# Two forgetting-attention heads by halves of their queries, with the first merged half's projection beside them

## The chip, the cores and the metric

One core of a Trainium2 chip runs the kernel. A time is the device time of one execution in microseconds. The engines are TensorE (PE, with its weight loads as PEld), VectorE (DVE), ScalarE (ACT), GpSimd (POOL) and SyncE (SP), which issues the DMA transfers. Each engine runs its own list of instructions in order and waits on semaphores for the others.

## The reference

A decoder block on 2048 tokens with 1024 channels in float32: a token mixer and a SwiGLU FFN. The change is in the token mixer, whose core is this:

```python
def token_mixer(h, w_in, b_forget, w_up_a, w_up_b, w_out):
    z = h @ w_in
    qa, ka, va, qb, kb, vb, fz, gza, gzb = jnp.split(z, SPLIT_POINTS, axis=-1)
    ya = dilated_mixture(qa, ka, va) @ w_up_a
    yb = forgetting_attention(qb, kb, vb, fz, b_forget) @ w_up_b
    merged = jax.nn.sigmoid(gza) * ya + jax.nn.sigmoid(gzb) * yb
    return merged @ w_out
```

Branch A (`dilated_mixture`) has 12 heads of 64 channels in three groups; each query sees a short band of keys, and the three groups are merged with weights made from their softmax denominators. Branch B (`forgetting_attention`) has 4 heads of 64 channels; each query sees all keys up to its own, with a bias that is a running sum of log forget gates. So of a head of branch B the second half of the queries needs all keys, the first half only the first half of them.

## The kernel before

float32 products are made of parts: a factor is split into a high and a low part (`split`, L106 on ACT for the high part, L107 on DVE for the low one), and `mm3` takes three products (L100, L101, L102). After the input projection the scheduler of the program gets five pieces of work in this order, as generators that yield after each step:

- `branch_a` (L711): 12 heads, each in four units of 512 queries: scores (L754, L758), eviction with bias and running maximum (L760), exponential (L768), transposes (L785), products with the values (L796), output rows `utok` (L808), stored to `u_scr`. With the last unit the softmax statistics of the group go out, and come back as `md`.
- `branch_b` (L912): heads 0 to 3, each whole (`head_f`, L820). A head loads queries `qs`, keys `kh` and `kl` (1 MB each) and values `vhl` (1 MB) through `head_tiles`, and has eight units of 256 queries (`cq`), of two blocks each. `scores(cq, b)` makes the products with the keys in segments of up to 512 (L850), the eviction with the bias `bi` (L852) and the exponential (L862). `sums(cq)` makes transposes (L886), splits them (`ph` by ACT, `pl` by DVE), and multiplies with the values (L894). Every second unit stores its 512 queries to `u_scr` and adds one to `f_done`.
- `merge_weights` (L946): the weights of branch A's three groups, on DVE and ACT, stored to `w_scr` (in the trace `wrow<-mw`, L970).
- `up(0)` and `up(1)` (L972): the projection of the first and the second half of the tokens. The first part builds the operand `y`: for each of four 128-row blocks it loads branch outputs (`uw<-u`, L981) and weights spread over partitions (`uw<-wrow` and `uw<-rc`, L987) into a `uw` tile, multiplies (L989), adds the groups (L991) and splits. The pool `bigx` holds three `uw` tiles, so the fourth load waits until the first tile has been used. The second part takes eight column blocks with 48 products each of 512 columns (L100 to L102, `psZ<-y,wu`), then multiplies with the gates (`gt`, L1014), adds and stores.

The multiplies and adds of the first part are put on engines by two tables, `UM` and `UA`: of 24, 14 run on POOL and 10 on DVE. `together` (L1018) interleaves generators by a virtual clock, one step of the one that is furthest behind, with a factor for each. First come branch A (`PACE[0]` = 0.6) and branch B; when A ends, `merge_weights`; then branch B alone until `f_done` is 14, which is when the first half of head 3's queries is done; then `up(0)` (`PACE[1]` = 0.6) beside what is left of head 3; then what is left of `up(0)`, and `up(1)`. This is the order in which work is given to the scheduler; it moves instructions on each engine by its own estimates, so that the order on an engine is to be read from the built program.

Of the kernel before, what the change touches and what calls it, by code (L numbers as in the profile page):

```python
# [11 lines left out]
F32R = mybir.dt.float32r  # L12
I32 = mybir.dt.int32
AF = mybir.ActivationFunctionType
ALU = mybir.AluOpType
# [3 lines left out]
P = 128  # L19
T = 2048  # L20
D = 1024
NT = T // P
# [27 lines left out]
UT = (("pc",), ("wh", "wl"))  # L50
UM = ("GVGG", "GVGV")
UA = ("GG", "VV")

PACE = (0.6, 0.6)

# [4 lines left out]
def trunk(ctx, tc, x, c, w_ada, b_ada, norm_mix, w_in, b_forget, w_up_a, w_up_b, w_out,  # L60
# [19 lines left out]
    def slot(tag, name, shape=None, dt=F32):  # L80
        kib, n = SLOTS[tag]
        return (sv if tag == "mid" else sb).tile(shape or [P, kib * 256], dt, tag=tag, name=name, bufs=n)
# [4 lines left out]
    def raw(t):  # L87
        return t.bitcast(F32)
# [580 lines left out]
    nev = [0]  # L669

    def head_tiles(qj, kj, half, vj, sl, d):

        r = []
        for n, j, part in (("qs", qj, 0), ("kh", kj, 0), ("kl", kj, 1)):
            r.append(slot("big", n, dt=F32R))
            to, src = raw(r[-1]), qk_scr[j][half, part:part + 2].rearrange("a p t -> (a p) t")
            if n == "qs" and d == 16:

                for c_ in range(NCH):
                    SP.dma_start(to.rearrange("p (r c n) -> p c r n", c=NCH, r=16)[:, c_],  # L680
                                 src[:, c_ * CH:(c_ + 1) * CH].rearrange("p (r n) -> p r n", r=16))
            else:
                SP.dma_start(to, src)
        full = vj < 3
        if full:
            vhl = slot("mid", "va", [P, NT, 65])
            G.memset(vhl[:, :, 64:65], 1.0)
        else:
            vhl = slot("big", "vhl", [P, NT, P], F32R)
        src = v_scr[vj][:, sl, :]  # L690
        dst = vhl[:, :, :64] if full else raw(vhl)
        if d == 1:
            SP.dma_start(dst, src.rearrange("(n i) e -> i n e", i=P))
        else:
            src = src.rearrange("(n i r) e -> n i r e", r=d, i=P)
            dst = dst.rearrange("p (r n) e -> n p r e", r=d)
            for n in range(NT // d):
                SP.dma_start(dst[n], src[n])
        return (*r, vhl)

# [118 lines left out]

    def head_f(h):  # L820
        qs, kh, kl, vhl = head_tiles(12 + h // 2, 14 + h // 2, h % 2, 3, h, 1)
        nf = [slot("mid", "nf") for _ in range(2)]
        for i in range(2):
            SP.dma_start(nf[i], brow(nf_scr[h, i * D:(i + 1) * D], D, P))
        uy, den, Ls = [None], {}, {}

        def scores(cq, b):
# [7 lines left out]
            for i, sg in enumerate(segs):  # L835
# [13 lines left out]
                for j, kk in enumerate((kh, kl)):  # L849
                    PE.matmul(s[:, :e - sg], qs[:, qb * P:(qb + 1) * P], kk[:, sg:e],  # L850
                              start=(j == 0), stop=(j == 1))
# [14 lines left out]
        def sums(cq):  # L866
# [9 lines left out]
            for kp in range(cq + 1):  # L876
# [14 lines left out]
                for i, kb in enumerate((2 * kp, 2 * kp + 1)):  # L891
                    q0 = P if last and i == 1 else 0
                    for j, p_ in enumerate(ops):
                        PE.matmul(uo[:, q0:256], vhl[:, kb, :], p_[:, 256 * i:256 * i + 256 - q0],  # L894
                                  start=(kp == 0 and i == 0 and j == 0),
                                  stop=(last and i == 1 and j == 1), skip_group_check=True)
            if cq % 2 == 0:
# [14 lines left out]
    def branch_b():  # L912

        behind = None
        for h in range(NHB):
            scores, sums = head_f(h)
            for cq in range(8):
                for b in range(2):
                    scores(cq, b)
                    yield (2 * cq + b + 1) / 4 * 0.7  # L920
                    if b == 0 and behind:
                        yield from behind()
                behind = lambda sums=sums, cq=cq: sums(cq)
            if h == NHB - 1:
                yield from behind()
    f_end, f_done = [None], [0]

# [44 lines left out]
    def up(cp):  # L972
# [3 lines left out]
        for p_ in range(4):  # L976
            acc = None
            for g in range(3 if p_ < 2 else 1):
# [7 lines left out]
                for i in range(2):  # L986
                    SP.dma_start(wb[64 * i:64 * i + 64, :],  # L987
                                 bass.AP(tensor=src.tensor, offset=src.offset + i * T, ap=[[0, 64], [1, D]]))
                (V if UM[cp][g + (p_ > 1) * 3] == 'V' else G).tensor_tensor(uu, uu, wb, op=ALU.mult)  # L989
                if acc is not None:  # L990
                    (V if UA[cp][g - 1] == 'V' else G).tensor_tensor(uu, uu, acc, op=ALU.add)  # L991
                acc = uu
            for c_ in range(2):
                split(y[c_][0][:, p_, :], y[c_][1][:, p_, :], acc[:, c_ * CH:(c_ + 1) * CH])
            yield 3.0
        for j in range(KT):
# [6 lines left out]
            for c_ in range(2):  # L1003
# [5 lines left out]
                for i, gt in enumerate(gts):  # L1009
                    o = ps("Z")  # L1010
                    for k in range(2 * i, 2 * i + 2):
                        mm3(o, w[:, 0, k, :], w[:, 1, k, :], yh[:, k, :], yl[:, k, :], k == 2 * i,
                            k == 2 * i + 1)
                    V.tensor_tensor(gt, o, gt, op=ALU.mult)  # L1014
# [16 lines left out]
    merge_weights()  # L1031
    together([(gb, 1.0)], lambda: f_done[0] >= 4 * (NHB - 1) + 2)
    tt_only[0] = "U"
# [181 lines left out]
```

## Time and profile before

| what | us |
|---|---|
| median of 3 runs | 2899.26 |
| lowest and highest run | 2895.91, 2902.61 |
| the profiled execution's own time | 2897.54 |
| its span, first to last instruction | 2895.8 |
| input projection, up to the first attention product | 0 to 880 |
| branches A and B beside each other | 880 to 1178.4 |
| branch B alone | 1178.4 to 1257.8 |
| `up(0)` beside the rest of head 3 | 1257.8 to 1342.7 |
| rest of `up(0)` and `up(1)` | 1342.7 to 1418.4 |
| output projection and FFN | 1418.4 to 2895.8 |

The bounds of the stages are the ends and starts of groups of PE's instructions: the last product of branch A (L796), the first of `up(0)` (L100), the last with branch B's values (L894) and the last of `up(1)` (L102). The table is read with the page's share of PE, which is busy for nearly the whole span, and with the busy time and granted clock by stage.

### The profile page before, as it was taken

The page shows a single profiled execution, that of the slowest core. Times are in us where ns is not written, and L with a number is a line of the kernel's source. Part 1 is how long each engine was busy: PE and PEld are TensorE (multiplying, and loading weights), DVE is VectorE, ACT ScalarE, POOL GpSimd, SP SyncE. Part 2 cuts the span into 40 slices and gives each one's busy share as a digit, 9 for nine tenths or more (in the row PEclk, how much of TensorE's full clock was granted, in tenths as well). Part 3 has the DMA queues.
Part 4 walks back from the last instruction along what each step waited for, and adds up shares of the span by engine and source line. Part 5 has one row for each costly group of instructions (what it writes and reads, how often), then busy time and mean ns, then how long its engine had stood idle before and what let it go on. Part 6 is the DMA issues. An engine that isn't in the chain of part 4 may idle for free.

```text
span 2895.8 us, 40840 instructions
## 1 busy us (share of the span) xinstructions
PE 2774.1 (96%) x13778; PEld 2309.5 (80%) x13778; DVE 2041.0 (70%) x4269; ACT 1376.4 (48%) x2726; POOL 213.9 (7%) x305
## 2 busy tenths in 40 slices
PE   7999999999999999888899999999999999989998
PEld 6789888978887878666677788888888888868876
DVE  5865578576646887687967766657755558795987
ACT  4654335344447777653356533335333335343543
POOL 0000000000002222563200000000000000000000
PEclk9999999999999999998999999999999999999999
DMA  7687466467757668569766554444522235785642
GB/s 242 166 226 220 131 207 204 148 168 212 235 176 261 239 176 259 144 176 310 265 211 207 189 178 138 135 146 137 164 86 79 83 109 179 217 264 168 219 155 99
DMA packets 520858, 530.52 MB, mean 183 GB/s; under 512 B 91556, under 2 KB 372540, under 8 KB 514236
## 3 DMA queue, kind: packets, MB, share of 16 engines
q1 hardware_dynamic: 520648, 527.91, 58.6%
q8 instruction: 108, 1.77, 0.3%
q14 instruction: 102, 0.84, 0.1%
HBM read 356.51 MB, written 171.29 MB: 182 GB/s over the span
## 4 chain that ended last, share of the span: by engine, by line
PE 47%; DVE 3%; ACT 1%; DMA 1%; issue 1%; DVEq 0%; ACTq 0%
PE psX L100 9%; PE psX L101 9%; PE psX L102 9%; PE psZ L100 4%; PE psZ L101 4%; PE psZ L102 4%; PE psY L101 2%; PE psY L102 2%; PE psY L100 2%; DVE wl L107 0%; DVE wt L217 0%; PE psT L1090 0%; ACT wh L106 0%; ACT u L244 0%; DMA wr<-act 0%
## 5 line engine op out<-in xcount | busy, mean ns | idle before, releaser
L106 ACT ACTIVATE wh<-wt 128x512 fp32r<-128x512 f32 (+1 forms) x464 | 288.5, 623 | 637.0 <-PE psX L101 344.6
L107 DVE TENSOR_TENSOR wl<-wt,wh 128x512 fp32r<-128x512 f32 (+1 forms) x464 | 314.6, 681 | 257.8 <-ACT wh L106 240.6
L106 ACT ACTIVATE wh<-wr 128x512 fp32r<-128x512 f32 (+1 forms) x324 | 201.5, 623 | 433.1 <-PE psX L101 239.1
L107 DVE TENSOR_TENSOR wl<-wr,wh 128x512 fp32r<-128x512 f32 (+1 forms) x324 | 220.0, 680 | 200.9 <-ACT wh L106 183.2
L217 DVE TENSOR_TENSOR wt<-wr 128x512 f32<-128x512 f32 (+1 forms) x216 | 146.5, 678 | 12.0 <-DMA wr<-in_w_in_dram 5.1
L217 DVE TENSOR_TENSOR wt<-wr,wt 128x512 f32<-128x512 f32 (+1 forms) x216 | 147.8, 684 | 3.8
L244 ACT ACTIVATE u<-psX 128x512 f32<-128x512 f32 x216 | 125.3, 580 | 8.1 <-PE psX L102 8.1
L838 POOL TENSOR_SCALAR bi<-nf,F_col 128x512 f32<-128x512 f32 (+3 forms) x160 | 104.9, 658 | 229.3 <-DVE mx L852 192.3
L862 ACT ACTIVATE L<-L,nmf 128x512 f32<-128x512 f32 (+3 forms) x160 | 103.1, 647 | 20.7 <-DVE nmf L858 20.5
L894 PE MATMUL psY<-ph,vhl 128*128 128x256 f32 (+1 forms) x288 | 82.4, 299 | 9.1 <-ACT ph L106 7.8
L1120 DVE TENSOR_TENSOR ac<-psZ,u 128x512 f32<-128x512 f32 x88 | 60.4, 687 | 42.2 <-PE psZ L102 41.2
L894 PE MATMUL psY<-pl,vhl 128*128 128x256 f32 (+1 forms) x288 | 81.8, 312 | 7.8 <-DVE pl L107 6.8
L106 ACT ACTIVATE ph<-psT 128x512 fp32r<-128x512 f32 (+1 forms) x101 | 56.2, 568 | 53.5 <-PE psT L886 53.3
L796 PE MATMUL psY<-pf,va 128*65 128x128 f32 (+1 forms) x408 | 77.7, 324 | 1.3 <-DVE pf L792 0.9
L760 DVE CUSTOM_DVE_ANT_0 L<-psX,bias 128x128 f32<-128x128 f32 (+1 forms) x192 | 64.6, 357 | 19.8 <-PE psX L758 14.1
L107 DVE TENSOR_TENSOR pl<-psT,ph 128x512 fp32r<-128x512 f32 (+1 forms) x101 | 64.5, 646 | 16.2 <-ACT ph L106 16.0
L768 ACT ACTIVATE L<-L,nm 128x128 f32<-128x128 f32 (+1 forms) x192 | 72.1, 450 | 5.5 <-DVE nm L763 4.5
L100 PE MATMUL psZ<-y,wu 128*128 128x512 f32 x128 | 55.7, 435 | 18.7 <-DVE gt L1014 11.5
L100 PE MATMUL psX<-f_A11h,wh 128*128 128x512 f32 x176 | 69.4, 394 | 0.0
L894 PEld LDWEIGHTS psY<-ph,vhl 128*128 128x128 f32 x288 | 56.7, 197 | 15.6 <-ACT ph L106 10.9
L102 PE MATMUL psX<-f_A11h,wl 128*128 128x512 f32 x176 | 69.1, 393 | 0.0
L101 PE MATMUL psX<-f_A11l,wh 128*128 128x512 f32 x176 | 69.1, 392 | 0.0
(536 smaller groups left out, 8732.6 us busy)
## 6 DMA issues: line engine op xcount, KB each, us to landing
x<-x SPq DMA_DIRECT2D x192, 256.0 KB
wr<-in_w_ffn_in_dram SPq DMA_DIRECT2D x88, 512.0 KB
wr<-in_w_in_dram SPq DMA_DIRECT2D x64, 512.0 KB
qk<-sh SPq DMA_DIRECT2D x192, 128.0 KB
act<-ac SPq DMA_DIRECT2D x88, 256.0 KB
pc<-wfg SPq DMA_DIRECT2D x77, 256.0 KB
qk<-st SPq DMA_DIRECT2D x128, 128.0 KB
wa<-in_w_ada_dram SPq DMA_DIRECT2D x64, 256.0 KB
```

The source lines that it names most:

```text
L100: PE.matmul(o, lh, rh, start=first, stop=False, skip_group_check=True)
L101: PE.matmul(o, lh, rl, start=False, stop=False, skip_group_check=True)
L102: PE.matmul(o, ll, rh, start=False, stop=last, skip_group_check=True)
L106: A.activation(hi, src, AF.Copy)
L107: V.tensor_tensor(lo, src, raw(hi), op=ALU.subtract)
L217: V.tensor_tensor(v[i], *made[i](g, v), op=ALU.subtract)
L244: A.activation(t, o, AF.Copy, scale=1.0 if scale is None else scale)
L768: A.activation(Lb(b, o0, 256), Lb(b, o0, 256), AF.Exp, bias=nm[:, bb:bb + 1])
L796: PE.matmul(uo[:65, qb_[0] * P:qb_[0] * P + w], va[:, 4 * u + kb_, :], pf[:, pos:pos + w], start=i_ == 0, stop=i_ == len(runs) - 1, skip_g ...
L838: G.tensor_scalar(bi[:, :e - sg], nf[sg // D][:, sg % D:sg % D + e - sg], 1.0, F_col[:, qb * NHB + h:qb * NHB + h + 1], op0=ALU.mult, op1= ...
L862: A.activation(Ls[cq, b, sg][:, :e - sg], Ls[cq, b, sg][:, :e - sg], AF.Exp, bias=nm, accum_out=dp[:, i:i + 1])
L894: PE.matmul(uo[:, q0:256], vhl[:, kb, :], p_[:, 256 * i:256 * i + 256 - q0], start=(kp == 0 and i == 0 and j == 0), stop=(last and i == 1 ...
```

## The change

Branch B is given in six pieces instead of four: heads 0 and 1 whole, then the first halves of the queries of heads 2 and 3, then their second halves. A first half loads 1024 queries and 1024 keys, two operands to a tile (`kk`, `qv`); a second half loads the other 1024 queries and all keys and values again. Heads 2 and 3 so load 5.5 MB each in place of 4 MB. `up(0)` may start when `f_done` is 12, with both first halves done, and runs beside both second halves; its factor `PACE[1]` is 1.25 in place of 0.6, and a step of its first part counts 4.0 in place of 3.0. The tables `UM` and `UA` go: all 24 multiplies and adds of the `uw` tiles run on DVE. The first products of `up(0)` (`cp + j + c_ + k == 0`) are held in the order behind the last product with branch B's values that has been given so far.

```diff
-PACE = (0.6, 0.6)
+PACE = (0.6, 1.25)
+
+FOX = ((None, 0), (None, 1), (0, 2), (0, 3), (1, 2), (1, 3))
...
+    def half_tiles(h, part):
+
+
+        qj, kj, half, n = 12 + h // 2, 14 + h // 2, h % 2, D if part == 0 else T
+        if part == 0:
+            t = [slot("big", "kk", dt=F32R), slot("big", "qv", dt=F32R)]
+            kh, kl = [t[0][:, i * D:(i + 1) * D] for i in range(2)]
+            qs, vhl = t[1][:, :D], t[1][:, D:].rearrange("p (n e) -> p n e", e=P)
+        else:
+            kh, kl, qs, vhl = [slot("big", nm, dt=F32R) for nm in ("kh", "kl", "qs", "vhl")]
+            qs, vhl = qs if part is None else qs[:, :D], vhl.rearrange("p (n e) -> p n e", e=P)
+        SP.dma_start(raw(qs), qk_rows(qj, half, 0)[:, D if part else 0:n])
+        for i, kk in enumerate((kh, kl)):
+            SP.dma_start(raw(kk), qk_rows(kj, half, i)[:, :n])
+        SP.dma_start(raw(vhl), v_scr[3][:n, h, :].rearrange("(n i) e -> i n e", i=P))
+        return qs, kh, kl, vhl
...
-                        PE.matmul(uo[:, q0:256], vhl[:, kb, :], p_[:, 256 * i:256 * i + 256 - q0],
-                                  start=(kp == 0 and i == 0 and j == 0),
-                                  stop=(last and i == 1 and j == 1), skip_group_check=True)
+                        f_pe[0] = PE.matmul(uo[:, q0:256], vhl[:, kb, :], p_[:, 256 * i:256 * i + 256 - q0],
+                                            start=(kp == 0 and i == 0 and j == 0),
+                                            stop=(last and i == 1 and j == 1), skip_group_check=True).ins
...
-        for h in range(NHB):
-            scores, sums = head_f(h)
-            for cq in range(8):
+        for part, h in FOX:
+            scores, sums = head_f(h, part)
+            for cq in range(4 if part else 0, 4 if part == 0 else 8):
...
-            if h == NHB - 1:
+            if (part, h) in (FOX[-1], FOX[-3]):
                 yield from behind()
-    f_end, f_done = [None], [0]
+                behind = None
+    f_end, f_done, f_pe = [None], [0], [None]
...
-                (V if UM[cp][g + (p_ > 1) * 3] == 'V' else G).tensor_tensor(uu, uu, wb, op=ALU.mult)
+                V.tensor_tensor(uu, uu, wb, op=ALU.mult)
                 if acc is not None:
-                    (V if UA[cp][g - 1] == 'V' else G).tensor_tensor(uu, uu, acc, op=ALU.add)
+                    V.tensor_tensor(uu, uu, acc, op=ALU.add)
...
-            yield 3.0
+            yield 3.0 if cp else 4.0
...
-                        mm3(o, w[:, 0, k, :], w[:, 1, k, :], yh[:, k, :], yl[:, k, :], k == 2 * i,
-                            k == 2 * i + 1)
+
+                        with tc.issue_after(f_pe[0]) if cp + j + c_ + k == 0 else nullcontext():
+                            mm3(o, w[:, 0, k, :], w[:, 1, k, :], yh[:, k, :], yl[:, k, :], k == 2 * i,
+                                k == 2 * i + 1)
...
-    together([(gb, 1.0)], lambda: f_done[0] >= 4 * (NHB - 1) + 2)
+    together([(gb, 1.0)], lambda: f_done[0] >= 12)
```

PE runs 13470 instructions in both programs. Three places show what moved. The first is PE after branch A's last product. Before, a stretch of head 2 and 3, with products of queries and keys (L850, `psX<-kh,qs`), transposes (L886) and products with the values (L894):

```order
L894 MATMUL psY_13261<-ph_13340,vhl_12332 128x256
L886 MATMUL psT_13432<-ident_73,L_13194 128x128
L886 MATMUL psT_13432<-ident_73,L_13355 128x128
L886 MATMUL psT_13432<-ident_73,L_13194 128x128
L886 MATMUL psT_13432<-ident_73,L_13355 128x128
L850 MATMUL psX_13557<-kh_12328,qs_12326 128x512
L850 MATMUL psX_13557<-kl_12330,qs_12326 128x512
L886 MATMUL psZ_13497<-ident_73,L_13211 128x128
```

After, the end of the first half of head 3 and the first products of head 2's second half, whose keys and queries are the tiles `kh_13535`, `kl_13536` and `qs_13537`:

```order
L910 MATMUL psY_13454<-ph_13498,qv_12972 128x256
L910 MATMUL psY_13454<-pl_13499,qv_12972 128x256
L910 MATMUL psY_13454<-ph_13498,qv_12972 128x128
L910 MATMUL psY_13454<-pl_13499,qv_12972 128x128
L866 MATMUL psX_13552<-kh_13535,qs_13537 128x512
L866 MATMUL psX_13559<-kh_13535,qs_13537 128x512
L866 MATMUL psX_13552<-kl_13536,qs_13537 128x512
L866 MATMUL psX_13559<-kl_13536,qs_13537 128x512
```

Between branch A's last product and these products with the keys PE now has 52 instructions, transposes and products of head 3's first half; nothing of a second half stands among them, and nothing of `up(0)`.

The second place is SP's list of DMA issues from the weights of branch A on. Before, the loads of `up(0)` and the stores of head 3 (`u_202`, `rc`), with no load of a head among them:

```order
L970 DMA wrow<-mw 128x64 x3
L987 DMA uw<-wrow 64x1024 x6
L906 DMA u_202<-uy 64x512
L981 DMA uw<-u_196 128x1024
L987 DMA uw<-wrow 64x1024 x2
L981 DMA uw<-u_198 128x1024
L987 DMA uw<-wrow 64x1024 x2
L981 DMA uw<-u_200 128x1024
L987 DMA uw<-wrow 64x1024 x2
L981 DMA uw<-u_201 128x1024
```

After:

```order
L922 DMA u_202<-uy 64x512
L988 DMA wrow<-mw 128x64 x3
L1005 DMA uw<-wrow 64x1024 x6
L999 DMA uw<-u_196 128x1024
L1005 DMA uw<-wrow 64x1024 x2
L999 DMA uw<-u_198 128x1024
L1005 DMA uw<-wrow 64x1024 x2
L710 DMA qs<-qk_124 128x1024
L712 DMA kh<-qk_126 128x2048
L712 DMA kl<-qk_126 128x2048
L713 DMA vhl<-v_130 128x16x128
L999 DMA uw<-u_200 128x1024
```

The loads of head 2's second half now stand behind the stores of the weights and behind the fourth and fifth load of a `uw` tile, which need a free one of the three.

The third place is DVE at the end of `merge_weights`. Before, splits (`pl`) and evictions (L852) of head 2 and 3 follow:

```order
L969 TENSOR_TENSOR mw<-mw 128x64 x3
L864 TENSOR_REDUCE den<-dp 128x1
L902 TENSOR_TENSOR uy<-psY,ulf 64x256
L107 TENSOR_TENSOR pl<-psT,ph 128x512
L107 TENSOR_TENSOR pl<-psZ,ph 128x512
L107 TENSOR_TENSOR pl<-psT,ph 128x512 x2
L852 ISA L,mx<-psZ,bi,mx 128x512
```

After, eight operations on `uw` tiles and two splits of `y` come ahead of the next eviction:

```order
L987 TENSOR_TENSOR mw<-mw 128x64 x3
L1007 TENSOR_TENSOR uw<-uw 128x1024 x2
L1009 TENSOR_TENSOR uw<-uw 128x1024
L1007 TENSOR_TENSOR uw<-uw 128x1024
L1009 TENSOR_TENSOR uw<-uw 128x1024
L107 TENSOR_TENSOR y<-uw,y 128x512 x2
L1007 TENSOR_TENSOR uw<-uw 128x1024 x2
L1009 TENSOR_TENSOR uw<-uw 128x1024
L868 ISA L,mx<-psX,bi 128x512
```

By stage, with the same bounds as in the table above, PE's instructions stand so in the two lists (products of 512 columns of the projections, of queries and keys with 512 columns and with fewer, products with the values, transposes, others):

| stage | before | after |
|---|---|---|
| A and B beside each other | 1815 in all | 1833 in all |
| from A's end to the first product of `up(0)` | 0, 44, 24, 141, 129, 5: 343 | 0, 34, 10, 72, 60, 3: 179 |
| to the last product with B's values | 144, 32, 6, 107, 99, 2: 390 | 156, 54, 14, 164, 157, 3: 548 |
| to the last product of `up(1)` | 266 (240 of `up`, 26 of the output projection) | 254 (228 and 26) |

## Rows read from the trace of the kernel before

**Rows 1.** The page's head: span, and busy time with share of the span and instructions of each engine.

```profile
span 2895.8 us, 40840 instructions
...
PE 2774.1 (96%) x13778; PEld 2309.5 (80%) x13778; DVE 2041.0 (70%) x4269; ACT 1376.4 (48%) x2726; POOL 213.9 (7%) x305
```

**Rows 2.** Busy time by stage. Columns: the stretch, its length in us, then busy us (and count) of PE, PEld, DVE, ACT and POOL, the granted clock of PE, the share of DMA and GB/s.

```profile
880.00:1178.40 298.40, 283.20 (x1998) 244.87 (x1997) 240.69 (x942) 232.56 (x558) 82.36 (x164) 1.00 0.71 223
1178.40:1257.80 79.40, 60.79 (x346) 49.64 (x344) 59.12 (x170) 46.52 (x119) 50.24 (x58) 0.89 0.42 110
1257.80:1342.70 84.90, 72.26 (x392) 59.92 (x390) 68.44 (x137) 40.48 (x94) 43.28 (x38) 0.94 0.88 263
1342.70:1418.40 75.70, 66.70 (x269) 50.73 (x268) 61.27 (x87) 21.48 (x36) 29.46 (x20) 0.95 1.00 343
```

**Rows 3.** Instructions by source line on PE: count, min/median/max in ns, first start and last end in us, forms.

```profile
L796 PE MATMUL psY<-pf,va x408: 270/273/432, 895.6 to 1178.4; 128*65 128x128 f32 x72, 128*65 128x256 f32 x64
...
L894 PE MATMUL psY<-pl,vhl x288: 272/282/583, 894.9 to 1342.7; 128*128 128x256 f32 x144
...
L100 PE MATMUL psZ<-y,wu x128: 388/395/797, 1257.8 to 1417.9; 128*128 128x512 f32 x128
...
L102 PE MATMUL psZ<-y,wu x128: 387/393/628, 1260.3 to 1418.3; 128*128 128x512 f32 x128
```

**Rows 4.** PE's timeline in the second and third stage: start, duration of one, and so the distance from one start to the next.

```profile
1182.51 0.28 PE L894 MATMUL psY<-pl,vhl 128*128 128x256 f32 x1
1182.63 0.28 PE L894 MATMUL psY<-ph,vhl 128*128 128x256 f32 x1
1182.75 0.49 PE L886 MATMUL psT<-ident,L 128*128 128x128 f32 x3
1182.99 0.36 PE L894 MATMUL psY<-pl,vhl 128*128 128x256 f32 x1
...
1308.90 0.40 PE L101 MATMUL psZ<-y,wu 128*128 128x512 f32 x1
1309.13 0.39 PE L102 MATMUL psZ<-y,wu 128*128 128x512 f32 x1
1309.36 0.40 PE L850 MATMUL psX<-kh,qs 128*128 128x512 f32 x1
1309.60 0.40 PE L850 MATMUL psX<-kl,qs 128*128 128x512 f32 x1
1309.83 0.27 PE L894 MATMUL psY<-ph,vhl 128*128 128x256 f32 x1
```

**Rows 5.** Timeline of all engines from branch A's end: the last output rows of branch A, the stores of the weights, their loads, the first multiplies on POOL and on DVE (start, duration, idle time of the engine ahead of it and what ended it). "SPq" is the DMA queue.

```profile
1179.36 1.03 ACT L808 ACTIVATE utok<-psY 65x512 f32<-65x512 f32 x1
...
1190.36 1.27 SPq L970 DMA_DIRECT2D wrow<-mw  x3
...
1191.81 3.66 SPq L987 DMA_DIRECT2D uw<-wrow  x6
...
1196.70 2.40 POOL L989 TENSOR_TENSOR uw<-uw 128x1024 f32<-128x1024 f32 x1 [9.23 <-issue]
...
1199.00 1.23 DVE L989 TENSOR_TENSOR uw<-uw 128x1024 f32<-128x1024 f32 x1 [1.00 <-DMA uw<-wrow]
```

**Rows 6.** Instructions on the `uw` tiles: count, min/median/max in ns, first start and last end in us.

```profile
L987 SPq DMA_DIRECT2D uw<-wrow x24: 445/541/882, 1191.8 to 1308.1; - x24
L981 SPq DMA_DIRECT2D uw<-u x16: 320/358/1583, 1165.1 to 1350.1; - x16
L989 POOL TENSOR_TENSOR uw<-uw x10: 2345/2382/2847, 1196.7 to 1316.1; 128x1024 f32<-128x1024 f32 x10
L989 DVE TENSOR_TENSOR uw<-uw x6: 1203/1278/2032, 1199.0 to 1357.1; 128x1024 f32<-128x1024 f32 x6
```

**Rows 7.** DMA issues: names, queue, count, KB each.

```profile
kh<-qk SPq DMA_DIRECT2D x16, 1024.0 KB
...
kl<-qk SPq DMA_DIRECT2D x16, 1024.0 KB
...
uw<-u SPq DMA_DIRECT2D x16, 512.0 KB
...
uw<-wrow SPq DMA_DIRECT2D x24, 256.0 KB
```

**Rows 8.** PE's waits from 1257.8 to 1342.7 us: the waiting instruction's tile and line, the releaser, and the total in us, the count and the longest.

```profile
PE psZ L100 <- DVE gt L1014: 6.0, 3, 4.6
PE psZ L100 <- ACT wu L106: 3.0, 1, 3.0
PE psY L894 <- DVE pl L107: 2.3, 4, 0.9
PE psZ L102 <- DVE wu L107: 0.7, 1, 0.7
PE psZ L100 <- ACT y L106: 0.7, 1, 0.7
```

**Rows 9.** Groups on DVE from 1178.4 to 1418.4 us, shapes apart: count, busy us, mean ns of one, then idle time ahead of them and what ended it.

```profile
L107 DVE TENSOR_TENSOR pl<-psT,ph 128x512 fp32r<-128x512 f32 x41 | 27.3, 679 | 3.0 <-ACT ph L106 3.0
...
L107 DVE TENSOR_TENSOR y<-uw,y 128x512 fp32r<-128x512 f32 x16 | 14.9, 956 | 3.8 <-ACT y L106 3.7
```

More of the change, by code (lines that the diff above doesn't have):

```diff
@@ L1 @@
-from contextlib import ExitStack
+from contextlib import ExitStack, nullcontext
 import numpy as np
@@ L50 @@
 UT = (("pc",), ("wh", "wl"))
-UM = ("GVGG", "GVGV")
-UA = ("GG", "VV")
-PACE = (0.6, 0.6)
+PACE = (0.6, 1.25)
+FOX = ((None, 0), (None, 1), (0, 2), (0, 3), (1, 2), (1, 3))
 THIRDS = ((0, 3), (6, 4), (14, 4))
@@ L669, in trunk, with qk_rows @@
     nev = [0]
+    def qk_rows(j, half, part):
+        return qk_scr[j][half, part:part + 2].rearrange("a p t -> (a p) t")
     def head_tiles(qj, kj, half, vj, sl, d):
@@ L675, in head_tiles @@
             r.append(slot("big", n, dt=F32R))
-            to, src = raw(r[-1]), qk_scr[j][half, part:part + 2].rearrange("a p t -> (a p) t")
+            to, src = raw(r[-1]), qk_rows(j, half, part)
             if n == "qs" and d == 16:
@@ L683, in head_tiles @@
                 SP.dma_start(to, src)
[L684 to L691, printed above, removed]
+        va = slot("mid", "va", [P, NT, 65])
+        G.memset(va[:, :, 64:65], 1.0)
+        src, dst = v_scr[vj][:, sl, :], va[:, :, :64]
         if d == 1:
@@ L698, in head_tiles @@
                 SP.dma_start(dst[n], src[n])
-        return (*r, vhl)
+        return (*r, va)
+    def half_tiles(h, part):
[12 more added lines that the diff above has]
+        return qs, kh, kl, vhl
     base = cst.tile([P, 256], F32, name="base")
@@ L818, in head_a, with head_f @@
         return scores, sums
[L820 to L823, printed above, removed]
+    def head_f(h, part):
+        qs, kh, kl, vhl = half_tiles(h, part)
+        q_off = 8 if part else 0
+        nf = [slot("mid", "nf") for _ in range(1 if part == 0 else 2)]
+        for i in range(len(nf)):
             SP.dma_start(nf[i], brow(nf_scr[h, i * D:(i + 1) * D], D, P))
@@ L849, in scores @@
                 for j, kk in enumerate((kh, kl)):
-                    PE.matmul(s[:, :e - sg], qs[:, qb * P:(qb + 1) * P], kk[:, sg:e],
+                    PE.matmul(s[:, :e - sg], qs[:, (qb - q_off) * P:(qb - q_off + 1) * P], kk[:, sg:e],
                               start=(j == 0), stop=(j == 1))
```

## The prediction

> **What bounds the kernel now.** I read the page's head first: PE is busy for 96% of the span, no other engine for more than 70% [rows 1]. So the time is PE's work plus PE's gaps, and an edit that adds no PE work can only move gaps. The windows by stage say where they are [rows 2]. While A and B run beside each other PE is busy for 283.2 of 298.4 us at a granted clock of 1.00. Then come three stages, bounded by PE's groups [rows 3]: branch B alone, 60.8 of 79.4 us, clock 0.89; `up(0)` beside the rest of head 3, 72.3 of 84.9, clock 0.94; the rest of the projection, 66.7 of 75.7, clock 0.95. The reader is to see that the first of the three is the poorest, and that DMA is not short there (110 GB/s, against 343 in the third). These 240.0 us are what the change can move.
>
> Busy time of pipelined matmuls overlaps, so I price PE's work by the distance of starts in a dense stretch [rows 4]: 0.23 us for a product of the projection (512 columns), 0.24 for queries by keys with 512 columns, 0.12 for one with the values (I take that for short key products too), 0.24 for three transposes, so 0.08. With the counts of the order (table by stage above) the first stage holds 44×0.24 + 24×0.12 + 141×0.12 + 129×0.08 + 0.5 = 41.2 us, the second 144×0.23 + 32×0.24 + 6×0.12 + 107×0.12 + 99×0.08 + 0.2 = 62.4, the third 266×0.23 = 61.2. What is left is stall: 38.2 us, 22.5 and 14.5, or 0.111, 0.058 and 0.055 us for each instruction. The sum of stalls is 75.2; all that follows is about whether it grows or shrinks.
>
> **The change part by part.** *Work.* PE's instructions are as many as before, and at these distances the new stages hold 23.1 us (34, 10, 72, 60, 3), 83.2 (156, 54, 14, 164, 157, 3) and 58.4 (254): 164.7, where before there were 164.8. 18 instructions more lie ahead of A's end, at about 0.1 us: +1.8.
>
> *First stage.* Before it has 343 instructions, then 179; at the same stall of 0.111 for each, 19.9 us in place of 38.2. This is where the change gains: less of branch B runs alone.
>
> *The hole.* It does not run through, though. PE has 52 instructions after A's end that depend on nothing new; at the stage's own pace (79.4 us for 346 [rows 2], 0.23 for each) they last 12 us from A's last product, to about 10 us after the last `utok` row ends at 1180.4 [rows 5]. Then PE stands before products whose keys are loaded by SP behind the stores of the weights and two `uw` loads that need a tile freed by DVE. How long that takes is read from the same chain in the trace: from `utok`'s end to the first multiply on a `uw` tile 16.3 us [rows 5]. The load for the fifth tile needs DVE to be through the first five operations, at 1.24 us each about 6.2 (the median is 1.28, the fastest 1.20) [rows 6]. SP then issues that tile and the head's operands, about 1.8 us by the medians of DMA issues of this size (0.36 + 2×0.54 [rows 6], and 0.36 for the queries, an estimate). 1 MB of the tile, 0.5 of queries, 1 and 1 of keys [rows 7] at the 343 GB/s of the third stage [rows 2] are 10.2 to 10.7 us. So the keys are there 16.3 + 6.2 + 1.8 + 10.7 = 35.0 us after `utok`'s end and PE stands for 25. Nothing else covers it: `up(0)` needs the same `uw` tiles and is queued behind. The bounds: 17, if the load is let go after the third operation and the first product needs only the queries and high keys (3.7 in place of 6.2, 5.8 of data in place of 10.7); 30, if the first multiply comes at 1199.0, as DVE's first did, rather than at 1196.7 [rows 5], and the data at the 263 GB/s of the second stage [rows 2] (+2.3 and +2.6). I take 25. A negative cost is excluded here, since before the change PE has head 3's products to do there.
>
> *Second stage.* 548 instructions, of which 156 of the projection and 392 of branch B. The trace shows PE waiting on gates and operands of the projection for 10.4 us and on `pl` for 2.3 [rows 8]. By their kinds: 10.4×156/144 = 11.3, 2.3×392/246 = 3.7, and the 9.8 us that no wait explains (small gaps and the clock of 0.94) stay: 24.8. The bounds are far apart. Below: the mix of A and B ran with 5% of gaps (283.2 of 298.4 [rows 2]), which is 83.2/0.95 − 83.2 = 4.4 us. Above: today's second stage by instruction, 548×0.058 = 31.8. I take 24.8, near the upper end, since its rows are of the same two kinds of work on the same pools.
>
> *Third stage.* 254 of 266 instructions: 13.8 us of stall.
>
> *POOL's operations.* 14 operations go from POOL (about 2.38 us) to DVE (about 1.24) [rows 6]: DVE gets 17 us more, POOL loses 33. DVE was busy 188.8 of these 240.0 us [rows 2]; with 206 it has still 40 us free in all, so I give the move no cost of its own, beside the five operations in the hole. The cover is thin in the second stage, where DVE has 68.4 of 84.9 us and gets the evictions and splits of 146 instructions of branch B more; if it is gone, the cost is what DVE lacks there, under 10 us, and lies within the upper bound above. A small gain is possible: `y` splits take 956 ns where splits of the same size take 679 [rows 9], 16×0.28 = 4.4 us of DVE if POOL's share in `uw` was the reason. I count none of it.
>
> *The wait behind B's products.* It keeps the first product of `up(0)` behind what has been given of B. What is queued behind it is the rest of the projection; the instructions ahead of it are branch B's, which PE has to run anyway. Today's wait of that first line on gates is 6.0 us in three waits [rows 8], and none of them is removed by a later place. I price it at 0, between a loss of the 0.7 us that one wait for `y` takes [rows 8] and a gain of the same.
>
> *Extra loads.* 3 MB more; the first halves' share falls beside A and B (DMA share 0.71), the second halves' into a stage with 263 GB/s where 343 are to be had [rows 2]. At nothing, beside the hole.
>
> **Sum.** Stalls 19.9 + 25 + 24.8 + 13.8 = 83.5 against 75.2: +8.3; work −0.1 + 1.8. Together +10 us. The profiled execution took 2897.5 us, 1.7 below the median, so the sum gives 2907.5 from it and 2909.2 from the median; I say 2908. With the bounds of the hole (−8, +5) and of the stall by instruction (+7), less a few us for DVE's splits, this case covers 2897 to 2918.
>
> **Rivals.** *A: mixing works, and the kernel is faster.* Mechanism: branch B's products fill the projection's waits for gates and operands, and the projection fills B's waits for evictions, so that the second stage runs as densely as A and B did. For it: PE at 95% in that mix, against 77% for B alone [rows 2]. Against it: the second stage is already such a mix and has only 85%. Price: 4.4 us of stall in place of 24.8, −20.4, so 2888, and 2880 with the hole at its lower bound. It decides once the second stage's stall is under about 15 us. Beside this stands a rule of the Trainium skill, "Perfetto Trace Analysis", section Optimization Strategy: where a kernel has regimes with different contended engines, interleaving the regimes may improve it. By that rule the sum would come out on A's side; the trace agrees for A with B, and only in part for the projection with B.
>
> *B: the queues entangle.* DVE and SP are each one list: a `uw` operation ahead of an eviction, and a load ahead of another, hold B and the projection up by turns. Then the second stage has its upper bound (+7) and the hole its own (+5): about 2920. For it: DVE's list after the weights, with eight operations on `uw` and two splits of `y` ahead of the next eviction. Against it: DVE has 20% to spare over the stage.
>
> *C: the hole is mostly covered.* The weights may come sooner than in the trace of before, since fewer of B's evictions stand among them on DVE, or the 52 instructions may start later; if 10 to 13 us of the hole go, the sum is about 0: 2898, no difference that shows. Against it: the chain from `utok` to the first multiply is mostly DMA, which the change doesn't shorten.
>
> **How the numbers follow.** A measurement of this kernel tells about 0.2%, 5.8 us, from no change. My case has 0.53 (of it 0.43 slower by more than that, 0.10 within), A 0.27 (0.23 faster, 0.04 within), B 0.12 (slower), C 0.08 (within). Faster 0.23, same 0.22, slower 0.55. The range reaches from A with a hole of about 19 us, 2882, past B's value to 2922; my case's own range is 2897 to 2918.
>
> **What would show it.** In the profile after: a gap of PE of 17 to 30 us, about 10 us after the last `utok`, ended by the keys' DMA, tells that the hole is there; a PE busy without it speaks for C. From the first product of `up(0)` to the last of B's values about 108 us with a PE share of 80 to 85% is my case, 88 us A, 115 us B. The third stage should take some 72 us. DVE's `uw` operations at 1.2 us and `y` splits near 0.7 would show POOL's share. I am wrong if the second stage is dense in spite of DVE's larger share of the work, or if the hole is filled by something that the order doesn't show.

## The result and the profile after

The changed kernel takes 2929.8 us (median of 4 runs, 2928.3 to 2932.1) against 2899.0 of the kernel before in the same runs: a ratio of 1.0104, interval 1.0091 to 1.0117, so about 31 us slower. The sign was forecast, the size was not: 2908, and the range ended at 2922. One execution among all that follow stands apart, with 4030 us in the experiment on early loads; without it the median there is 2905.2 in place of 2906.0.

By stage, with the bounds set by the same groups of PE as in [rows 2] and the same columns:

```profile
880.00:1179.80 299.80, 287.12 (x2020) 249.00 (x2019) 242.90 (x959) 234.26 (x564) 83.08 (x168) 0.99 0.68 209
1179.80:1187.80 8.00, 6.73 (x46) 5.32 (x44) 6.47 (x19) 5.71 (x14) 0.00 (x0) 1.00 0.37 72
1187.80:1216.50 28.70, 0.00 (x0) 0.00 (x0) 12.67 (x17) 1.53 (x3) 0.00 (x0) 0.57 0.80 228
1216.50:1256.40 39.90, 28.80 (x132) 21.38 (x133) 31.71 (x79) 22.17 (x55) 17.59 (x26) 0.80 1.01 308
1256.40:1375.70 119.30, 101.13 (x552) 84.86 (x551) 87.69 (x193) 57.11 (x136) 43.35 (x53) 0.91 0.57 173
1375.70:1450.40 74.70, 63.20 (x256) 46.39 (x256) 58.95 (x83) 21.92 (x37) 27.54 (x19) 1.00 1.00 341
```

The second to fourth row are the stage of branch B alone. In the third PE has no busy time at all for 28.7 us. The sum against [rows 2], on the spans 2927.8 and 2895.8:

| stage | before | forecast | after | after less before |
|---|---|---|---|---|
| A beside B (end of A) | 1178.4 | 1180.2 | 1179.8 | +1.4 |
| B alone, to the first product of `up(0)` | 79.4 | 68.0 | 76.6 | −2.8 |
| to the last product with B's values | 84.9 | 108.0 | 119.3 | +34.4 |
| rest of the projection | 75.7 | 72.2 | 74.7 | −1.0 |
| what follows | 1477.4 | 1477.4 | 1477.4 | 0.0 |

The gap itself: SP's timeline around it, with the first loads of head 2's second half (`qs`, `kh`, `kl`) in the last three rows,

```profile
1190.37 1.54 SPq L988 DMA_DIRECT2D wrow<-mw  x3
1192.32 3.66 SPq L1005 DMA_DIRECT2D uw<-wrow  x6
1201.68 0.33 SPq L999 DMA_DIRECT2D uw<-u  x1
1202.06 1.08 SPq L1005 DMA_DIRECT2D uw<-wrow  x2
1204.08 0.33 SPq L999 DMA_DIRECT2D uw<-u  x1
1204.74 1.08 SPq L1005 DMA_DIRECT2D uw<-wrow  x2
1205.94 0.52 SPq L710 DMA_DIRECT2D qs<-qk  x1
1206.55 0.38 SPq L712 DMA_DIRECT2D kh<-qk  x1
1207.02 0.38 SPq L712 DMA_DIRECT2D kl<-qk  x1
```

and PE's waits from 1179.8 to 1256.4 us, then from 1256.4 to 1375.7 (total, count, longest):

```profile
PE psX L866 <- DMA kh<-qk: 28.7, 1, 28.7
PE psX L866 <- DVE mx L868: 5.7, 7, 1.6
```

```profile
PE psX L866 <- DVE mx L868: 7.3, 6, 3.7
PE psZ L100 <- DVE gt L1034: 4.1, 2, 3.5
```

The reader is to see the chain that was read from [rows 5]: stores of the weights at 1190.4 (before 1190.4), the fifth tile's load at 1204.1, the keys behind it. The high keys are issued at 1206.6, 18.8 us into the gap, and PE starts 10 us after that. The waits on gates and operands of the projection, 10.4 us in [rows 8], have become fewer (6.4); a wait for evictions (`mx`) that the second stage did not have has come. DVE's waits there, 1256.4 to 1375.7 us, say why evictions are late, and its groups from 1179.8 to 1450.4 us (as [rows 9]) show the operations that came from POOL:

```profile
DVE uw L1007 <- DMA uw<-wrow: 9.5, 5, 4.5
...
DVE uw L1007 <- DMA uw<-rc: 2.0, 1, 2.0
```

```profile
L107 DVE TENSOR_TENSOR pl<-psT,ph 128x512 fp32r<-128x512 f32 x47 | 31.7, 681 | 7.1 <-ACT ph L106 6.9
L1007 DVE TENSOR_TENSOR uw<-uw 128x1024 f32<-128x1024 f32 x16 | 19.8, 1236 | 28.1 <-DMA uw<-wrow 23.7 <-DMA uw<-rc 3.0 <-DMA uw<-u 1.4
L107 DVE TENSOR_TENSOR y<-uw,y 128x512 fp32r<-128x512 f32 x16 | 10.6, 690 | 0.7 <-ACT y L106 0.7
```

DVE does 19.8 us of multiplies and stands idle for 28.1 us ahead of them, for transfers. 13.4 of these lie in PE's gap, where PE had no scores to evict. Behind the gap, while DVE stands, the evictions and splits of branch B that are behind it in its list stand too.

### The profile page after: what moved, and what is told of

Same layout as the page of the kernel before. It is cut to its first block, busy times and chain, and to the rows that moved or that the text cites. A ratio compares the mean times of both kernels' runs of the same rounds, so it can differ in the third digit from the quotient of the medians.

```text
span 2927.8 us, 40828 instructions
## 1 busy us (share of the span) xinstructions
PE 2776.7 (95%) x13778; PEld 2310.3 (79%) x13778; DVE 2050.0 (70%) x4283; ACT 1376.6 (47%) x2726; POOL 182.2 (6%) x291
## 4 chain that ended last, share of the span: by engine, by line
PE 45%; DVE 2%; DMA 2%; issue 1%; ACT 1%; POOLq 0%; DVEq 0%; SPq 0%; ACTq 0%
PE psX L100 9%; PE psX L101 9%; PE psX L102 8%; PE psZ L100 4%; PE psZ L101 4%; PE psZ L102 4%; PE psY L102 2%; PE psY L100 2%; PE psY L101 2%; DMA pc<-wfg 1%; PE psT L1110 0%; DVE wl L107 0%; DMA out_dram<-x 0%; ACT wh L106 0%; DVE wt L217 0%
## 5 line engine op out<-in xcount | busy, mean ns | idle before, releaser
L107 DVE TENSOR_TENSOR pl<-psT,ph 128x512 fp32r<-128x512 f32 (+1 forms) x110 | 70.5, 646 | 20.6 <-ACT ph L106 20.2
L775 DVE CUSTOM_DVE_ANT_0 L<-psX,bias 128x128 f32<-128x128 f32 (+1 forms) x192 | 64.1, 356 | 18.8 <-PE psX L773 14.1
L910 PE MATMUL psY<-pl,vhl 128*128 128x256 f32 x248 | 70.4, 311 | 6.6 <-DVE pl L107 5.7
L910 PE MATMUL psY<-ph,vhl 128*128 128x256 f32 (+1 forms) x248 | 72.0, 302 | 4.4 <-ACT ph L106 3.2
L783 ACT ACTIVATE L<-L,nm 128x128 f32<-128x128 f32 (+1 forms) x192 | 72.2, 450 | 5.5 <-DVE nm L778 4.7
L902 PE MATMUL psT<-ident,L 128*128 128x128 f32 x410 | 67.6, 285 | 1.8 <-DVE pl L107 1.8
```

The lines of the kernel that those rows point to most:

```text
L107: V.tensor_tensor(lo, src, raw(hi), op=ALU.subtract)
L783: A.activation(Lb(b, o0, 256), Lb(b, o0, 256), AF.Exp, bias=nm[:, bb:bb + 1])
L910: f_pe[0] = PE.matmul(uo[:, q0:256], vhl[:, kb, :], p_[:, 256 * i:256 * i + 256 - q0], start=(kp == 0 and i == 0 and j == 0), stop=(last a ...
```

## The experiments

Each kernel was measured in turns with the kernel before. First the two costs, each taken away from the changed kernel, then DVE's part put alone into the kernel before, then all but the halves.

**Early loads.** A second half's operands are given when head 3's first half begins:

```diff
+            if (part, h) == FOX[3]:
+                early[FOX[4]] = half_tiles(FOX[4][1], FOX[4][0])
```

> The changed kernel, but the operands of head 2's second half are loaded when the first half of head 3 begins, ahead of the weights of branch A and the projection's tiles in SP's list. Theory H (the order of loads makes the 28.7 us gap of PE): the gap goes, the first stage falls from 76.6 to about 50 us, the time to about 2904 (2900 to 2910). Rival S (PE then runs into the same evictions, splits and DVE operations a little sooner, and the time is only pushed into the second stage): the gap goes, but the second stage grows by 10 us or more, and the time is 2915 or above. A time under 2899 would say that the halves gain once the gap is gone.

Measured: 2906.0 us, 1.0029 (1.0018 to 1.0039) of the kernel before, 24 us under the changed one. Its stages from A's end (B alone, the second, the third):

```profile
1182.30:1222.40 40.10, 31.75 (x181) 24.76 (x180) 36.44 (x102) 26.75 (x69) 17.01 (x25) 0.91 0.66 186
1222.40:1348.90 126.50, 103.52 (x554) 83.84 (x553) 100.20 (x203) 58.21 (x136) 48.39 (x51) 0.93 0.82 239
1348.90:1425.80 76.90, 62.02 (x244) 46.05 (x244) 57.25 (x82) 20.81 (x36) 26.85 (x18) 0.96 0.92 314
```

No wait on keys is left. The first stage falls by 36.5 us, 7.8 more than the gap: for nearly as many instructions PE is busy 3.8 us less (clock 0.91, against 0.80 behind the gap), and the rest is shorter waits. 7 us come back in the second stage, 2 in the third and 2.5 ahead of A's end, about a third in all: theory H holds for the gap, with a part of what rival S said.

**POOL's operations back.** The tables `UM` and `UA` as before, all else as changed.

> The changed kernel with POOL's 14 multiplies and adds back by the old tables. If DVE's larger share in the second stage is what makes it 119.3 us, it falls by 5 to 10 us; but the operations ahead of the first loads then take POOL's 2.4 us each and the gap of PE grows by about 3 us. Theory H: within 5 us of the changed kernel, 2925 to 2935. Rival D (the move to DVE is the cost): 2920 or less.

Measured: 2921.3 us, 1.0076 (1.0061 to 1.0091), 8.5 us under the changed kernel. Its stage of B alone, and the second:

```profile
1180.90:1261.20 80.30, 36.36 (x186) 26.45 (x185) 40.99 (x109) 31.36 (x78) 45.73 (x40) 0.74 0.82 245
1261.20:1367.50 106.30, 96.05 (x544) 81.12 (x544) 84.17 (x185) 55.19 (x130) 50.73 (x53) 0.95 0.66 193
```

Its waits of PE, the gap first, then the longest two of the second stage:

```profile
PE psX L869 <- DMA kh<-qk: 32.9, 1, 32.9
```

```profile
PE psY L913 <- DVE pl L110: 4.7, 4, 2.5
PE psX L869 <- DVE mx L871: 1.8, 3, 0.8
```

The second stage falls from 119.3 to 106.3 us, the clock rises from 0.91 to 0.95, and the gap grows by 4.2: 32.9 us, one wait. All of PE's waits in the second stage are 9.7 us in place of 17.8, and PE is busy for 96.1 us in place of 101.1: these two make the 13 us. So the move costs 13 us in the second stage and gives 4 back in the gap. This lies between what the two theories said of the time; of the stage it is rival D's answer.

**DVE alone.** The kernel before with `V.tensor_tensor` for all 24 operations, no other edit.

> The kernel before with all multiplies and adds of the uw tiles on DVE, nothing else changed: that part alone. Theory H: little, -4 to +4 us against the kernel before (the operations are twice as fast, and the splits of y fall from 956 to about 690 ns, but DVE has 17 us more). Rival D: +8 us or more.

Measured: 2915.3 us, 1.0056 (1.0041 to 1.0071): +18 by the medians, +16 by the ratio. Theory H, that the move is nearly free, falls. DVE's waits from 1182 to 1357 us, then PE's:

```profile
DVE uw L989 <- DMA uw<-wrow: 16.1, 6, 5.9
...
DVE uw L989 <- DMA uw<-rc: 4.9, 2, 2.7
DVE uw L989 <- DMA uw<-u: 1.5, 1, 1.5
```

```profile
PE psX L850 <- DVE mx L852: 15.1, 9, 5.7
PE psY L894 <- DVE pl L107: 10.6, 6, 5.2
```

In the kernel before, the same lines from 1178.4 to 1342.7 us:

```profile
DVE uw L989 <- DMA uw<-wrow: 1.8, 2, 1.0
```

```profile
PE psY L894 <- DVE pl L107: 5.8, 8, 2.4
PE psX L850 <- DVE mx L852: 3.4, 4, 1.8
```

DVE's waits on these transfers are 22.5 us in place of 1.8, and PE waits 25.7 us on the two lines in place of 9.2. Of the 18.4 us between the two profiles 3.6 lie ahead of A's end, where both programs have the same instructions, and 10 in the stage of B alone. Behind that end the scheduler has moved instructions of PE, too, so the price is that of the move with the order made for it.

**All but the halves.** `FOX` with four whole heads and `f_done >= 14`, the rest as changed.

> All of the change but the halves: heads 2 and 3 whole, the projection's first half from the 14th store on, the factor 1.25, the step of 4.0, DVE for all uw operations, the first product behind the given products of branch B. Theory H: no gap of PE over 5 us on keys, and the time is near the kernel before, 2895 to 2905. If it is slower than 2910, the pace, the wait or DVE's share costs by itself.

Measured: 2922.3 us, 1.0079 (1.0064 to 1.0094). No wait on keys, and still +25: of that DVE's share alone is 18; factor, step and hold, the other 7, were not taken apart in this kernel. The halves themselves make the difference of 7.5 us to the changed kernel, gap and all.

**Both mends.** Early loads and POOL's operations back.

> The changed kernel with both: head 2's second half loaded early, and POOL's 14 operations back. If the gap on keys and DVE's list (its operations on uw tiles wait for DMA with evictions and splits of branch B queued behind) are two separate costs, they add: 24 us of the first and 8 to 13 us of the second below the changed kernel, 2892 to 2899, level with the kernel before or a little faster. Rival S (the halves themselves cost, by fewer PSUM buffers for scores and transposes beside the projection): 2902 or above.

Measured: 2898.9 us against 2897.5, 1.0002 (0.9993 to 1.0012). The two costs add up and make the whole loss: early loads give 24 us with DVE's operations and 22 with POOL's, POOL's operations 8.5 us with the gap and 7 without it. What is left of the change is worth nothing that can be told. The stages from A's end are 43.5, 114.1 and 78.3 us, 235.9 against 240.0 before, and A ends 6 us later, with 48 more PE instructions ahead of that end (925 from 1050 us to A's end, 877 before). The second of them:

```profile
1228.40:1342.50 114.10, 96.31 (x516) 77.74 (x517) 94.20 (x183) 55.28 (x127) 65.39 (x57) 0.94 0.85 252
```

**DVE's extra work without its waits**, tried in the kernel before:

```diff
+    def idle_ops(at_):
+        for i in range(3):
+            with tc.issue_after(at_):
+                V.tensor_tensor(base, base, base, op=ALU.max)
```

> The kernel before, POOL's operations kept, with three added DVE operations of 256 columns (about 0.4 us each) on a constant tile behind each of POOL's 14, which wait for no transfer: 17 us of DVE work as in the move, without its waits. Theory Q (DVE's list is held by waits for the uw transfers, 22 us in the run with DVE alone): the time grows by at most 6 us, 2897 to 2903. Rival W (DVE's work is what costs): +12 us or more, like the move itself (+17).

Measured: 2911.1 us, 1.0044 (1.003 to 1.0059): +13.5, rival W's number. But the experiment did not do what it was made for. The scheduler also moved DVE's own `uw` operations, and they now wait:

```profile
DVE uw L995 <- DMA uw<-wrow: 15.6, 4, 5.4
```

So work and waits came together, and it does not decide.

**Without the hold, and with the old pace**, each in the changed kernel.

> The changed kernel without the hold on the projection's first product. If the hold costs nothing, as the prediction has it, within 5 us of the changed kernel, 2925 to 2935, the gap on keys unchanged at about 28 us. If the first product waits in PE's list ahead of branch B's products now, slower by 5 us or more.

> The changed kernel with the old factor 0.6 and step 3.0. The projection is given faster, so more of it stands ahead of the second halves, and less is left beside the end of branch B. If the pace is a cost of the change, faster by 5 us or more, below 2925; if it mends something, slower than 2935; the prediction gave it no price, within 5 us.

Measured: 2927.8 (1.0105, 1.009 to 1.012) and 2930.2 us (1.0114, 1.0097 to 1.0131); the changed kernel had 1.0104. Neither is a cost there. With the old pace PE starts the projection 14 us sooner and ends the second stage 5 us later.

**Weights that lie ready.** To take the waits from DVE, the `uw` tiles multiply by rows of the denominators (`src = den_scr[HPG * g + 2 * p_, cs]`), once with DVE alone, once with POOL's share.

> The kernel before with all uw operations on DVE, and in place of branch A's merge weights the uw tiles multiply by rows of the softmax denominators, which lie in memory earlier; the merge weights are still made and stored, and their effect on the output is left out. DVE's work is that of the move, without the wait for the stores of the weights. To be read against the next kernel, the same without the move. Theory Q (waits at the head of DVE's list): at most 6 us above the next kernel. Rival W (DVE's work): 12 us or more above it.

> The kernel before, POOL's operations kept, with the rows of the denominators in place of branch A's merge weights in the uw tiles (the same part left out as in the kernel ahead). Both theories: within 6 us of the kernel before, since POOL's waits hold nothing of branch B.

Measured: 2911.2 (1.0044, 1.0029 to 1.0059) and 2903.9 us (1.0015, 1.0003 to 1.0026), 7 us apart, between the two theories. DVE's waits were not gone (`den` 14.0, `rc` 5.0, `u` 4.8 us): only three tiles can be loaded ahead, whatever the weights are. Not decided by this pair.

**The halves alone, with early loads**: POOL's operations, old pace, no hold.

> The halves alone with early loads of head 2's second half: POOL's 14 operations back, the factor 0.6 and the step 3.0 of the kernel before, no hold on the first product. If pace and hold are worth nothing, within 5 us of the run with them (2899), level with the kernel before; if they cost, 2893 or less, which would be faster than both kernels; if they help, 2904 or more.

Measured: 2923.3 us, 1.0085 (1.007 to 1.010), 24 us above the run with both mends. Without the hold, that program has the same order of instructions on PE, DVE and SP as with it, so the 24 us are the pace's. The second and third stage:

```profile
1225.90:1378.70 152.80, 119.18 (x566) 91.06 (x566) 99.16 (x194) 57.86 (x132) 68.48 (x61) 0.89 0.74 222
1378.70:1447.80 69.10, 51.25 (x208) 39.37 (x209) 51.45 (x74) 18.20 (x31) 22.12 (x15) 0.90 0.91 306
```

Together 221.9 us, against 192.4 with the factor 1.25. Pace (factor and step) is worth nothing while the gap and DVE's waits stand, and 24 us when they are gone.

**DVE's operations held back**: in the kernel before, with all of them on DVE, each multiply stands behind the evictions given so far (`with tc.issue_after(f_dv[0])`).

> The kernel before with all uw operations on DVE, each multiply held in the order behind the evictions of branch B given so far: the DVE work of the move, about 95 places later in DVE's list for the first of them. Theory Q (DVE's list is held by waits for the uw transfers): these waits fall from 22 us to under 6, PE's waits on splits and evictions from 26 us to about 10, and the time to 2897 to 2905. Rival W (the work itself): 2911 or more, with DVE busy where PE waits.

Measured: 2932.7 us, 1.0113 (1.0098 to 1.0129). Theory Q misses; the time lies in rival W's open range, but W does not say why the stage of B alone is back at 79.1 us (89.3 with the operations in their early place, 79.4 before). The third stage takes 93.2 us (77.8 with the early place), what follows is 15 us longer than before in a profiled execution that was 6 above the median, and some waits are left:

```profile
DVE uw L991 <- DMA uw<-wrow: 8.2, 5, 2.7
```

It shows that the place of these operations in DVE's list moves 10 us in or out of B's stage, not that waits are all of the cost.

**A longer pace** in the kernel with both mends, 1.75.

> The kernel with early loads and POOL's operations back (level with the kernel before), with the factor 1.75 in place of 1.25, so that the projection is given later beside the second halves. In that kernel the step from the old factor 0.6 to 1.25 was worth 24 us. If the trend goes on, 2890 or less, faster than both kernels; if 1.25 is near the best, 2896 to 2906.

Measured: 2904.3 us, 1.0018 (1.0009 to 1.0027). A longer pace than 1.25 gains nothing more; no version here beats the kernel before.

**Half of DVE's work, same places.**

```diff
-                V.tensor_tensor(uu, uu, wb, op=ALU.mult)
+                V.tensor_tensor(uu[:, :CH], uu[:, :CH], wb[:, :CH], op=ALU.mult)
```

> The kernel before with all uw operations on DVE, but each of them on 512 of the 1024 columns; the other half of the tile stays as loaded, so half of the merge's products and sums is left out. DVE's work on uw tiles is 24 operations of about 0.68 us, 16 us in all, against 30 in the run with whole operations and 12 on DVE in the kernel before; the operations stand at nearly the same places in DVE's list, and the transfers that they wait for are the same. Theory Q (waits at the head of the list): the waits stay above 15 us and the time stays 10 us or more above the kernel before, 2908 to 2917. Rival W (the work): the cost goes with the work, at most 6 us above the kernel before, 2896 to 2904.

Measured: 2911.1 us against 2897.8, 1.0049 (1.003 to 1.0068): +13 with half of the work, where whole operations gave +18. The operations take 692 ns at the median in place of 1224. DVE's waits and PE's from 1182 to 1357 us:

```profile
DVE uw L989 <- DMA uw<-wrow: 10.8, 5, 4.1
```

```profile
PE psY L894 <- DVE pl L107: 8.9, 8, 3.7
PE psX L850 <- DVE mx L852: 5.8, 7, 1.8
```

14 us less of DVE's work gives about 4 us back, and the two intervals overlap. By the sums of the expectation DVE has only 4 us more to do than in the kernel before, and still the kernel is 13 us slower. That speaks for theory Q in the time; its waits, 12.8 us with `rc` and `u`, came a little under the 15 that it named. But the stages do not bear it out as clearly: B alone takes 84.2 us, half way between 79.4 before and 89.3 (it holds 338, 346 and 361 of PE's instructions), and PE waits 14.7 us on the two lines, against 9.2 and 25.7. Behind A's end the profiles are about 8 us longer than before with half of the work and 15 with all of it. So work and waits are not told apart.

## Why the prediction was wrong

The direction and the first cause were right, the size was not. The forecast was +10, the profile shows +32.

*The hole* was right in its chain and nearly in its place and size. It was forecast about 10 us after `utok`, 25 us long between 17 and 30. In the trace after, the last `utok` row ends at 1182.2: the keys came 34.3 us behind it, where the sum had 35.0, but PE's own 52 instructions were through 5.6 us behind it, in 8.0 us and not in 12. So it came with 28.7. Without it the kernel is 24 us faster.

*First stage.* 76.6 in place of 68.0: 3.7 by the gap, 4.9 outside it. Ahead of the gap the 52 instructions took 4 us less than forecast, behind it the rest about 9 us more. Of the 39.9 us after the gap PE is busy for 28.8 at a granted clock of 0.80, where the stage before had 0.89. The windows show it closer:

```profile
1187.80:1192.00 4.20, 0.00 (x0) 0.00 (x0) 1.67 (x7) 0.38 (x1) 0.00 (x0) 0.98 0.58 168
1208.00:1216.50 8.50, 0.00 (x0) 0.00 (x0) 3.67 (x3) 0.00 (x0) 0.00 (x0) 0.50 1.03 343
1216.50:1220.00 3.50, 2.26 (x4) 1.00 (x4) 0.10 (x1) 0.00 (x0) 0.00 (x0) 0.50 1.05 361
1220.00:1225.00 5.00, 4.15 (x12) 2.93 (x12) 3.63 (x13) 1.90 (x6) 3.12 (x6) 0.50 1.07 314
1225.00:1230.00 5.00, 2.81 (x13) 1.85 (x12) 4.17 (x10) 2.50 (x7) 2.87 (x5) 0.84 1.04 426
```

A clock of 1.00 is 2.4 GHz, so the first 8.5 us after the gap ran at 1.2 GHz, right after PE had done nothing for 28.7 us. The sum took the old stall for each instruction and left this aftermath out. It is part of the 9 us, not all: with early loads PE is busy 3.8 us less in this stage.

*The step that failed* is "I give the move no cost of its own", POOL's operations. It was argued from DVE's free time: 206 of 240 us busy. The free time was there (DVE was busy for 87.7 of 119.3 us in the second stage after), but it did not make the move free. DVE's list runs in order; a multiply that waits for its tile (11.5 us in all in that stage) holds the evictions behind it, and PE's scores wait for these (7.3 us). In the kernel before, POOL waited 17.5 us for the same transfers, and of branch B only the bias tiles stood behind it, for which DVE waited 1.1 us. The runs give the move 18 us alone and 8.5 in the changed kernel (13 in the second stage, less 4 in the gap). That waits in DVE's list carry this cost is what the waits of PE and DVE point to, and is not shown: how much is wait, place or work stays open. The kernel with half the work kept 13 of the 18 us in the time, but about half behind A's end; no run took the waits away with the order kept, and holding the operations later cost as much elsewhere.

This step is not all of the 22 us between forecast and profile. With POOL's operations back the kernel is still 24 us slower than the one before, where the sum had 10: the gap is then 7.9 us longer than forecast (part of it by POOL's slower operations), the rest of the first stage 4.4 and the third stage 3.0. And without the hole the sum is −15 us, while the kernel with both costs gone is level. Its first stage is as forecast (43.5 us, the sum has 43.0), but A ends 4.7 us later than the sum has it, and the second and third stage take 6.1 us more each. So the gain of a shorter stage of B alone, 18 us in the sum, came back in the stages around it. Why is open. Early loads let more of branch B run ahead of A's end than the sum assumed, and some of A's end is chance: three of the programs have the same instructions up to there as the kernel before and end it 3.6 to 5.8 us later.

*The second stage's stall* was taken by kinds from [rows 8], 24.8 us with an upper bound of 31.8, and came to 36.1. With POOL's operations back the stage is 106.3 us, within 2 of the 108 forecast: in the changed kernel the excess is the failed step's. The term itself was not safe even so: with the gap gone as well the stage is 114.1 us. The upper bound fell, since it was read from a stage in which DVE waited 0.8 us for transfers. The waits of the projection that it scaled up became fewer, and waits on evictions took their place.

*Third stage and wait behind B's products.* 74.7 against 72.2; the hold is worth nothing, as forecast (−2 us without it). *POOL's share in `y`*: the splits fell from 956 to 690 ns [rows 9], the 4 us that were left out of the sum are real, and no run here shows what they are worth in the time.

*The rivals.* A did not come: in the second stage PE is busy for 101.1 of 119.3 us, 85%, as before. With POOL's operations back it is 96.05 of 106.3, 90%, but with the gap gone as well 96.31 of 114.1, 84%. The rule of the Trainium skill, "Perfetto Trace Analysis", section Optimization Strategy, that interleaving regimes may improve performance, is not borne out by these runs: none of the interleaved versions was faster than the kernel before. B was the nearest: it named DVE's list, with the operations on `uw` ahead of the next eviction, and spoke of holding by turns. It was priced at +7 for the second stage and had 0.12; the stage came 11.3 over the forecast. Its mechanism is the one that fits the waits best, and should have had the move's waits as a price of its own: the 14 operations that came from POOL, with loads into only three tiles. C did not come, since the chain from `utok` was not shorter (34.3 us, the sum has 35.0).

## What to carry to other kernels

An engine's free time in a window does not price an operation that waits for a transfer: ask what stands behind it in the list, and who waits for that. A slow engine on whose list little else waits can be the better place for such work; moving it to one that is twice as fast cost 18 us here. When work is cut in pieces so that something can start earlier, look where the loads of the next piece fall in the issuing queue: here the keys stood behind the weights and two loads that had to wait for a free tile, and 18.8 of the 28.7 us of the gap were over before they were issued. And count what comes back in the neighbouring stages: the stage of B alone fell by 36.5 us without the gap, the time by 24.

## What the runs showed of the hardware

DVE's split of `y` takes 956 ns on average in the kernel before, where POOL works on `uw` tiles beside it, 739 in the same kernel with all of these operations on DVE, and 690 in the changed one. With POOL's operations back in the changed kernel it takes 816, and 1308 with early loads besides:

```profile
L110 DVE TENSOR_TENSOR y<-uw,y 128x512 fp32r<-128x512 f32 x16 | 20.5, 1308 | 1.6 <-ACT y L109 1.6
```

The Trainium skill, "Perfetto Trace Analysis", section Optimizing Scalar/DVE Operations, reminds that GPSIMD and DVE share a read port of SBUF; these numbers agree with that, though no run here tells the port from other shared things.

PE's granted clock was 0.57 over the 28.7 us in which it had nothing to do and 0.80 over the next 39.9; the first 8.5 of these were at 0.50, the lower level. Without the gap that stage was 36.5 us shorter, more than the gap's length, and the time 24 us, less than it.
